# A two-half transformer layer on one core: from scheduled order to source order paced by an estimate

## The chip, the cores and the metric

The kernel runs on one core of a Trainium2 chip. The core has five engines that each work through a queue of their own: TensorE (PE in the profile: matmuls, with their weight loads shown apart as PEld), VectorE (DVE), ScalarE (ACT), GpSimd (POOL) and SyncE (SP, which here only issues transfers). An engine that reaches an instruction whose inputs aren't ready waits there, and everything behind it on the same queue waits too. The metric is device time in microseconds for one execution.

## What is computed

256 tokens of width 2048 pass through one layer of a hybrid decoder, all in f32:

```python
proj = rms_norm(x, g_mix_pre) @ w_in          # split into q, k, v, HGRN2 q/f/i/g and two gates
merged = sigmoid(gate_a) * (y_attn @ w_attn_branch) + sigmoid(gate_b) * (y_hgrn @ w_hgrn_branch)
x = x + rms_norm(merged @ w_out, g_mix_post)
gate, up = split(rms_norm(x, g_ffn_pre) @ w_gate_up)
x = x + rms_norm((silu(gate) * up) @ w_down, g_ffn_post)
ple_gate = sigmoid(rms_norm(x, g_ple_pre) @ w_ple_gate)
x = x + rms_norm((p @ w_ple_proj) * ple_gate, g_ple_post)
```

y_attn is sliding-window attention with sinks (16 heads, window 128), y_hgrn a gated linear recurrence (8 heads, chunks of 64). d_ff is 5632. Each weight matrix is read from HBM once, some 270 MB in all.

## The kernel before

The tokens are two halves of 128 (c = 0 and 1). The activations of a half are the stationary operand of a matmul, 128x128 and transposed, and the streamed weights are the moving one, 128x512. To keep f32 precision, every product is three matmuls in the fp32r format: xh·wh + xh·wl + xl·wh, where xh and wh are rounded values (`hi`, `wh`) and xl and wl the remainders (`lo`, `wl`). This gives 6192 "wide" matmuls and 584 small ones (128x128 transposes, the recurrence, the attention); the profile counts 814 small, since a product of plain f32 operands that isn't a transpose stands in it twice.

A weight **pair** is two chunks of 128 rows and 512 columns, 512 KB: SP loads it into one of 5 `raw` buffers, ACT writes `wh`, DVE writes `wl = raw - wh`; 8 pairs of split weights can be held. There are 516 pairs, each used by 12 wide matmuls, 6 for each half. `block` takes a slab of up to 8 pairs through half 0 (48 matmuls into one PSUM accumulator `acc`), then through half 1, then calls `evac`, which reads the accumulator on ACT or DVE.

The stages run in this order: 19 blocks of `w_in` (the mixer; the small matmuls of recurrence and attention stand among them), the two branch projections, `w_out`, `w_gate_up` in 11 pairs of blocks (ev_g and ev_u make `sg` = silu(gate)·up, which is transposed on PE into `actT`), `w_down`, and `w_ple_proj` with `w_ple_gate`. Three of the stages begin with a norm: at the start of the program, after w_out (the first norm boundary) and after w_down (the second). At a norm, `x` is updated on DVE, transposed on PE, multiplied by the gain into `hi` (ACT) and `lo` (DVE), and its sum of squares (ACT, `junk`) gives `rstd` (DVE, then a power on POOL). The scale by `rstd` is applied only when an accumulator of the next stage is read.

What sets the order: outside the first block the tile scheduler does. The source gives weight splits a higher priority (`AHEAD`) and the norms at the boundaries a higher one still (`URGENT`); PSUM is four `acc` banks, two `mt` and two `mh`. Only the first block's instructions are pinned in source order. There, x is loaded and transposed group by group (4 groups of 512 columns for each half), and a whole group is multiplied by its gains on DVE (`h`), rounded on ACT (`hi`) and subtracted on DVE (`lo`), each at 128x512.

Of the kernel before, what the change touches and what calls it, by code (L numbers as in the profile page):

```python
# [18 lines left out]
P = 128  # L19
# [8 lines left out]
AHEAD = 1000  # L28
URGENT = 3000
# [3 lines left out]
def block_kernel(ctx: ExitStack, tc: tile.TileContext, I, out: bass.AP):  # L33
    """256 tokens as two halves of 128 on the partitions; weights stream once.

    A product x @ w is xh@wh + xh@wl + xl@wh, with xh, wh the float32r
    roundings and xl, wl the remainders (exact in float32r).
    """
# [3 lines left out]
    wraw = ctx.enter_context(tc.tile_pool(name="wraw", bufs=5))  # L42
    wsplit = ctx.enter_context(tc.tile_pool(name="wsplit", bufs=8))
    psum = ctx.enter_context(tc.tile_pool(name="psum", bufs=4, space=bass.MemoryType.PSUM))

    V, A, G, T = nc.vector, nc.scalar, nc.gpsimd, nc.tensor
    count = [0]

# [4 lines left out]
    # 2 KB slots, handed out in the order of emission, the longest free first  # L53
# [14 lines left out]

    def acc():
        return psum.tile([P, NB], F32, tag="acc", name=nm("acc"))  # L70

    def misc(tag="mt"):
        return psum.tile([P, NB], F32, tag=tag, bufs=2, name=nm("misc"))

    pinned = [False]

    def kept(ins):
        return tc.keep_in_program_order(ins) if pinned[0] else ins

    def act(o, i, f, **kw):  # L80
        return kept(A.activation(o, i, f, **kw))  # L81

    def tt(o, a, b, op):
        return kept(V.tensor_tensor(o, a, b, op))  # L84

    def ts(o, a, s1, op0, s2=None, op1=None):
        if op1 is None:
            return kept(V.tensor_scalar(o, a, s1, None, op0))
        return kept(V.tensor_scalar(o, a, s1, s2, op0, op1))  # L89

    def stt(o, a, s, b, op0, op1):
        return kept(V.scalar_tensor_tensor(o, a, s, b, op0, op1))  # L92
# [8 lines left out]
    def weight_load(w, k, col):  # L101
        raw = wraw.tile([P, 2, NB], F32, tag="raw", name=nm("raw"))
        nc.sync.dma_start(
            raw, w[k * P:(k + 2) * P, col:col + NB].rearrange("(c p) n -> p c n", p=P))
        return raw

    def weight_split(raw):
        """hi and lo parts of two k-chunks."""
        hi = wsplit.tile([P, 2, NB], F32R, tag="wh", name=nm("wh"))
        lo = wsplit.tile([P, 2, NB], F32R, tag="wl", name=nm("wl"))  # L110
        act(hi, raw, AF.Copy)
        tt(lo, raw, hi.bitcast(F32), ALU.subtract)
        return [(hi[:, j, :], lo[:, j, :]) for j in range(2)]

    def weight_slab(w, ks, col):
        pairs = []
        for k in ks[::2]:
            raw = weight_load(w, k, col)
            with tc.high_priority(offset=AHEAD):
                pairs.append((k, weight_split(raw)))  # L120
        return pairs

    def products(ps, lhs, pairs, start=True, stop=True):
        n = len(pairs)
        for i, (k, parts) in enumerate(pairs):
            for j, (wh, wl) in enumerate(parts):
                xh, xl = lhs(k + j)
                T.matmul(ps, xh, wh, start=start and i == 0 and j == 0, stop=False)  # L128
                T.matmul(ps, xh, wl, start=False, stop=False)  # L129
                T.matmul(ps, xl, wh, start=False, stop=stop and i == n - 1 and j == 1)  # L130

    def block(w, ks, col, lhs, evac):
# [163 lines left out]
    for g in range(4):  # L296
        ahead = first_group(g + 1) if g < 3 else None
        if g == 1:
            lower_bounds()
# [623 lines left out]
```

## Time and profile before

| | |
|---|---|
| runs | 1552.91 us median of 3 (1552.19 to 1555.55) |
| profiled execution, first to last instruction | 1552.4 us |
| PE busy | 1516.8 us, 98% |
| weight loads busy | 1243.8 us, 80% |
| DVE busy | 889.8 us, 57% |
| ACT busy | 786.3 us, 51% |
| first wide matmul starts | 12.12 us |
| last wide matmul starts | 1542.06 us |

The profiled execution has no time of its own beside its span. The span lies inside the spread of the runs, 0.5 us below their median, so span and time are taken as one. The busy time of PE is modelled from pipelined matmuls that overlap (one is shown as 0.39 us long while the next starts 0.23 us later), so a slice with 98% busy can still hold lost time. What is lost is read from the starts: how many matmuls start in a stretch against how many could.

### The profile page before, as it was taken

The page shows a single profiled execution, that of the slowest core. Times are in us where ns is not written, and L with a number is a line of the kernel's source. Part 1 is how long each engine was busy: PE and PEld are TensorE (multiplying, and loading weights), DVE is VectorE, ACT ScalarE, POOL GpSimd, SP SyncE. Part 2 cuts the span into 40 slices and gives each one's busy share as a digit, 9 for nine tenths or more (in the row PEclk, how much of TensorE's full clock was granted, in tenths as well). Part 3 has the DMA queues.
Part 4 walks back from the last instruction along what each step waited for, and adds up shares of the span by engine and source line. Part 5 has one row for each costly group of instructions (what it writes and reads, how often), then busy time and mean ns, then how long its engine had stood idle before and what let it go on. Part 6 is the DMA issues. An engine that isn't in the chain of part 4 may idle for free.

```text
span 1552.4 us, 18678 instructions
## 1 busy us (share of the span) xinstructions
PE 1516.8 (98%) x7006; PEld 1243.8 (80%) x7006; DVE 889.8 (57%) x1228; ACT 786.3 (51%) x1052; POOL 24.4 (2%) x36
## 2 busy tenths in 40 slices
PE   7999999999999999999999999999999999999997
PEld 5778887887878888887888888888888888888886
DVE  6886748676445565556543553454446556654854
ACT  4755745555664433546443444344345545543852
POOL 2000000000000000000000000000000000000000
PEclk9999999999999999999999999999999999999998
DMA  7645454545336765545545654565565565755452
GB/s 245 230 135 191 129 197 139 187 129 196 110 109 210 247 211 173 193 153 196 200 162 180 217 174 168 200 219 180 172 215 190 190 195 180 246 184 179 171 179 98
DMA packets 146618, 282.54 MB, mean 182 GB/s; under 512 B 9136, under 2 KB 9600, under 8 KB 146528
## 3 DMA queue, kind: packets, MB, share of 16 engines
q1 hardware_dynamic: 145968, 280.33, 54.2%
q0 software_dynamic: 528, 1.01, 0.3%
q8 instruction: 55, 0.90, 0.2%
q14 instruction: 35, 0.29, 0.1%
q10 hardware_dynamic: 32, 0.01, 0.0%
HBM read 279.21 MB, written 2.10 MB: 181 GB/s over the span
## 4 chain that ended last, share of the span: by engine, by line
PE 83%; DMA 6%; ACT 4%; DVE 4%; issue 2%; POOL 0%; SPq 0%; POOLq 0%; ACTq 0%; DVEq 0%
PE acc L130 26%; PE acc L129 26%; PE acc L128 26%; DMA raw<-in_w_gate_up 3%; ACT wh L81 3%; PE misc L159 2%; DMA raw<-in_w_in 2%; DVE wl L84 2%; PE misc L478 1%; PE misc L599 1%; PE misc L617 1%; DVE sg L92 1%; DMA x<-in_x 1%; ACT junk L81 0%; DMA raw<-in_w_down 0%
## 5 line engine op out<-in xcount | busy, mean ns | idle before, releaser
L84 DVE TENSOR_TENSOR wl<-raw,wh 128x1024 fp32r<-128x1024 f32 x516 | 626.7, 1223 | 352.9 <-ACT wh L81 322.4
L129 PE MATMUL acc<-wl,hi 128*128 128x512 f32 x2064 | 809.7, 392 | 1.5 <-DVE wl L84 1.5
L128 PE MATMUL acc<-wh,hi 128*128 128x512 f32 x2064 | 809.4, 392 | 1.2 <-ACT hi L81 0.8
L130 PE MATMUL acc<-wh,lo 128*128 128x512 f32 x2064 | 809.1, 392 | 0.0
L81 ACT ACTIVATE wh<-raw 128x1024 fp32r<-128x1024 f32 x516 | 545.1, 1061 | 254.6 <-PE acc L130 182.1
L128 PEld LDWEIGHTS acc<-wh,hi 128*128 128x128 f32 x2064 | 388.1, 188 | 81.2 <-ACT hi L81 1.1
L129 PEld LDWEIGHTS acc<-wl,hi 128*128 128x128 f32 x2064 | 388.0, 188 | 80.9 <-DVE wl L84 2.1
L130 PEld LDWEIGHTS acc<-wh,lo 128*128 128x128 f32 x2064 | 388.0, 188 | 79.0 <-issue 0.5
L81 ACT ACTIVATE actT<-misc 128x512 f32<-128x512 f32 x22 | 13.2, 598 | 114.1 <-PE misc L159 114.1
L92 DVE SCALAR_TENSOR_TENSOR sg<-acc,rstd,sg 128x512 f32<-128x512 f32 x26 | 19.4, 747 | 77.4 <-PE acc L130 76.1
L81 ACT ACTIVATE sg<-acc,rstd 128x512 f32<-128x512 f32 x26 | 17.7, 681 | 84.1 <-PE acc L130 84.1
L84 DVE TENSOR_TENSOR lo<-actT,hi 128x512 fp32r<-128x512 f32 x44 | 30.2, 688 | 29.1 <-PE acc L129 22.1
L81 ACT ACTIVATE hi<-actT 128x512 fp32r<-128x512 f32 x44 | 27.4, 626 | 35.7 <-PE acc L130 29.8
L81 ACT ACT_TABLE_LOAD x30 | 38.5, 1283 | 2.1 <-PEq L911 1.2
L81 ACT ACTIVATE junk<-acc 128x512 bf16<-128x512 f32 x16 | 9.5, 596 | 56.2 <-DVE yg L84 56.2
L178 POOL TENSOR_TENSOR rstd<-mse,mhalf 128x1 f32<-128x1 f32 (+1 forms) x14 | 13.7, 979 | 1409.0 <-DVE mse L89 1409.0
L84 DVE TENSOR_TENSOR yg<-acc,gp 128x512 f32<-128x512 f32 x16 | 11.0, 686 | 42.7 <-PE acc L130 42.7
L81 ACT ACTIVATE xx<-xx 128x512 f32<-128x512 f32 (+1 forms) x28 | 16.7, 599 | 29.7 <-DVE xx L84 24.9
L81 ACT ACTIVATE gate<-acc,rstd 128x512 f32<-128x512 f32 x16 | 10.9, 681 | 35.1 <-PE acc L130 35.1
L605 DVE CUSTOM_DVE_ANT_0 s<-misc,amask 128x128 f32<-128x128 f32 (+1 forms) x32 | 10.1, 354 | 27.4 <-PE misc L599 27.4
L159 PE MATMUL misc<-ident,x 128*128 128x128 f32 x96 | 15.9, 296 | 8.8 <-DMA x<-in_x 6.7
L159 PEld LDWEIGHTS misc<-ident,x 128*128 128x128 f32 x96 | 11.6, 150 | 13.6 <-DMA x<-in_x 7.2
(157 smaller groups left out, 579.5 us busy)
## 6 DMA issues: line engine op xcount, KB each, us to landing
raw<-in_w_gate_up SPq DMA_DIRECT2D x176, 512.0 KB, 5.1
raw<-in_w_in SPq DMA_DIRECT2D x152, 512.0 KB, 5.1
raw<-in_w_down SPq DMA_DIRECT2D x88, 512.0 KB, 5.5
raw<-in_w_out SPq DMA_DIRECT2D x32, 512.0 KB, 5.5
raw<-in_w_ple_gate SPq DMA_DIRECT2D x32, 512.0 KB, 5.8
raw<-in_w_attn_branch SPq DMA_DIRECT2D x16, 512.0 KB, 5.9
raw<-in_w_hgrn_branch SPq DMA_DIRECT2D x16, 512.0 KB, 5.6
x<-in_x SPq DMA_DIRECT2D x16, 256.0 KB, 6.9
```

The costliest lines, as they stand in the source:

```text
L81: return kept(A.activation(o, i, f, **kw))
L84: return kept(V.tensor_tensor(o, a, b, op))
L92: return kept(V.scalar_tensor_tensor(o, a, s, b, op0, op1))
L128: T.matmul(ps, xh, wh, start=start and i == 0 and j == 0, stop=False)
L129: T.matmul(ps, xh, wl, start=False, stop=False)
L130: T.matmul(ps, xl, wh, start=False, stop=stop and i == n - 1 and j == 1)
L159: T.transpose(ps[:, cols(i)], src[:, cols(i)], ident)
L178: G.tensor_tensor(r, u, mhalf[:, :m], ALU.pow)
L478: T.matmul(ps[:, cols(h, 64)], xh, blk(xh)[:, :, 1, :], start=True, stop=True)
L599: T.matmul(ps[:, cols(i, nk * P)], qT[:, cols(j0 + i)], kTp[n][:, g, 0:nk * P], start=True, stop=True)
L605: V.tensor_tensor_reduce(s[:, cols(i, nk * P)], ps[:, cols(i, nk * P)], amask[:, (1 - c) * P:256], 1.0, NEG, ALU.add, ALU.max, mx[:, hb + ...
L617: T.matmul(y[:, cols(hb + i, 64)], pT[:, cols(i * nk + b)], vtok[:, b, kv:kv + 64], start=b == 0, stop=b == nk - 1)
```

## The change

Every instruction of every engine is now kept in the order in which the Python source emits it. The source emits in an order that it works out itself: a running clock counts 0.227 us for each wide matmul and 0.11 us for each small one, each of the other engines has an estimate of when it will be free, and everything that isn't a product of streamed weights is written as a generator that yields what it waits for (an engine, a tile, or a number of microseconds). A generator that is due by the clock is stepped between the matmuls (`pump`), or at once where something needs its result (`hurry`). Weight splits are paced too (`prefetch`): one pair at least 2.3 us after the last, up to 7 pairs ahead, up to 13 around the norm boundaries and in the ple stage.

Within a block the halves now alternate pair by pair: 6 matmuls for half 0, then 6 for half 1. Only at the two norm boundaries (last block before, first block after) and in the last block is half 1 six pairs behind half 0 (`LAG`), and while half 1 finishes the last block before a norm, splits beyond two pairs pause (`calm`). The 8 PSUM banks come from one pool. The products p @ w_ple_proj are computed first of all, stored to DRAM by POOL's queue (8 transfers of 256 KB) and read back through SP's queue after w_down. In the first block each group of x is now made by chunk: 4 times 128x128 `hi` on ACT, then 4 times `lo` on DVE, with no `h`. The order of some mixer blocks, the order of the three terms (xh·wh, xl·wh, xh·wl), and a few loads of ACT's tables ahead of their use change as well. The numbers of wide and small matmuls and of pairs stay as they were.

```diff
-AHEAD = 1000
-URGENT = 3000
+SPLIT, LOADED, PACE = 7, 5, 2.3
+EXTRA = 6
+LAG = 6
+WIDE, SMALL = 0.227, 0.11
+LATENCY = 0.2
...
+            start = max([clock[0], self.until] + [written.get(key(x), 0.0) for x in outs + ins])
+            self.until = start + us
+            for x in outs:
+                written[key(x)] = self.until + LATENCY
...
+                return tc.keep_in_program_order(f(o, *a, **kw))
...
+    V = InOrder(nc.vector, 0.08, 0.00105)
+    A = InOrder(nc.scalar, 0.16, 0.00095)
...
+    def step(gen):
+        to = next(gen, None)
+        if to is not None:
+            if to is T:
+                due = clock[0] + 0.2 + LATENCY
+            elif isinstance(to, InOrder):
+                due = max(clock[0], to.until) + LATENCY
+            elif hasattr(to, "shape"):
+                due = max(clock[0], written[key(to)])
+            else:
+                due = clock[0] + to
+            count[0] += 1
+            heapq.heappush(waiting, (due, count[0], gen))
...
+    def pump():
+        while waiting and waiting[0][0] <= clock[0]:
+            step(heapq.heappop(waiting)[2])
...
-    def block(w, ks, col, lhs, evac):
-        pairs = weight_slab(w, ks, col)
-        for c in range(2):
-            ps = acc()
-            products(ps, lhs[c], pairs)
-            evac(c, ps)
...
+    def prefetch():
+
+        while loaded and (len(ready) < 2 or (
+                not calm[0] and len(ready) + held[0] < depth[0] and clock[0] > paced[0])):
+            paced[0] = max(paced[0], clock[0] - PACE) + PACE
+            split_pair()
+            if plan:
+                load_pair()
...
+        for i in range(n + lag):
+            if lag and i in (lag, n):
+                calm[0] = i == n and last
+            if i < n:
...
+                use(0, i)
+                prefetch()
+                pump()
+            if i >= lag:
+                use(1, i - lag)
+                pairs[i - lag][1]()
+                held[0] -= 1
+                prefetch()
+                pump()
...
-            if not by_chunk:
-                h = slot("h")
-                tt(heads(h), heads(ps), gcol[:, c0:c0 + 4].unsqueeze(2).broadcast_to([P, 4, P]), ALU.mult)
-                self.groups.append(split(h))
...
+    prefetch()
+    for n in range(4):
+        stream([acc(), acc()], [p_lookup(0), p_lookup(1)], "w_ple_proj", [0, 1], n * NB, evac=ev_p(n))
+        if n in (0, 2):
+            add_xg(n // 2)
...
+    first = [acc(), acc()]
     for g in range(4):
+        for h in range(2):
+            stream(first, hT, "w_in", [4 * g + 2 * h, 4 * g + 2 * h + 1], 5 * NB, g + h == 0, g + h == 4)
+            if g in (1, 2) and h == 0:
+                add_xg(g + 1)
...
+        block("w_gate_up", K16, j * NB, h2T, ev_g, LAG * (j == 0))
+        depth[0] = SPLIT
+        block("w_gate_up", K16, DFF + j * NB, h2T, ev_u)
...
+    for n in range(4):
+        block("w_ple_gate", K16, n * NB, h3T, ev_s(n), LAG * (n in (0, 3)))
```

What moves is shown at three places in the order in which each engine has its instructions. The numbers in the names only tell buffers apart.

**The first block.** DVE, before: while the first block of w_in runs, the third group of x follows the splits `wl` of the second, each group as `h`, then `lo`.

```order
L84 TENSOR_TENSOR h_54_217<-misc_53_212,gcol_73 128x512
L84 TENSOR_TENSOR lo_56_220<-h_54_217,hi_55_219 128x512
L84 TENSOR_TENSOR wl_58_224<-raw_50_206,wh_57_223 128x1024
L84 TENSOR_TENSOR wl_60_228<-raw_51_208,wh_59_227 128x1024
L84 TENSOR_TENSOR h_62_236<-misc_61_231,gcol_73 128x512
L84 TENSOR_TENSOR lo_64_239<-h_62_236,hi_63_238 128x512
```

DVE after, at the third group of x (`lo_121` is of half 0, `lo_126` of half 1):

```order
L132 TENSOR_TENSOR wl_105_373<-raw_67_222,wh_104_372 128x1024
L132 TENSOR_TENSOR wl_108_385<-raw_75_253,wh_107_384 128x1024
L132 TENSOR_TENSOR wl_119_423<-raw_91_304,wh_118_422 128x1024
L132 SCALAR_TENSOR_TENSOR lo_121_428<-misc_110_390,gcol_104,hi_114_403 128x128 x4
L132 TENSOR_TENSOR wl_123_440<-raw_97_327,wh_122_439 128x1024
L132 SCALAR_TENSOR_TENSOR lo_126_446<-misc_112_395,gcol_104,hi_116_408 128x128 x4
L132 TENSOR_TENSOR wl_128_458<-raw_102_355,wh_127_457 128x1024
```

ACT after, at the same place:

```order
L132 ACTIVATE wh_107_384<-raw_75_253 128x1024
L132 ACTIVATE hi_114_403<-misc_110_390,gcol_104 128x128 x4
L132 ACTIVATE hi_116_408<-misc_112_395,gcol_104 128x128 x4
L132 ACTIVATE wh_118_422<-raw_91_304 128x1024
L132 ACTIVATE wh_122_439<-raw_97_327 128x1024
```

A group's `hi` for both halves now stands on ACT ahead of the next `wh`, and on DVE the `wl` of that pair stands ahead of the group's `lo`, while before `lo` stood ahead of the `wl`s.

**The transposes of sg in gate_up.** PE, before: `acc_1465` is the last accumulator of an up block (half 0), `acc_1468` that of the next block; `misc_1467` receives the four transposes of `sg_1438`.

```order
L130 MATMUL acc_1465_7142<-wh_1463_7138,lo_1146_5548 128x512
L128 MATMUL acc_1468_7199<-wh_1442_7096,hi_1164_5629 128x512
L129 MATMUL acc_1468_7199<-wl_1443_7097,hi_1164_5629 128x512
L130 MATMUL acc_1468_7199<-wh_1442_7096,lo_1165_5630 128x512
L128 MATMUL acc_1468_7199<-wh_1442_7096,hi_1164_5629 128x512
L129 MATMUL acc_1468_7199<-wl_1443_7097,hi_1164_5629 128x512
L159 MATMUL misc_1467_7193<-ident_71,sg_1438_7041 128x128 x4
L130 MATMUL acc_1468_7199<-wh_1442_7096,lo_1165_5630 128x512
```

PE after: `acc_1905` and `acc_1906` are the halves of an up block, `acc_1933` and `acc_1934` those of the next.

```order
L132 MATMUL acc_1905_7332<-wh_1907_7346,lo_1586_5853 128x512
L132 MATMUL acc_1905_7332<-wl_1908_7347,hi_1585_5848 128x512
L132 MATMUL acc_1906_7333<-wh_1907_7346,hi_1628_6014 128x512
L132 MATMUL acc_1906_7333<-wh_1907_7346,lo_1629_6019 128x512
L132 MATMUL acc_1906_7333<-wl_1908_7347,hi_1628_6014 128x512
L132 MATMUL acc_1906_7333<-wh_1907_7346,hi_1628_6014 128x512
L132 MATMUL acc_1906_7333<-wh_1907_7346,lo_1629_6019 128x512
L132 MATMUL acc_1906_7333<-wl_1908_7347,hi_1628_6014 128x512
L132 MATMUL acc_1933_7480<-wh_1910_7364,hi_1563_5762 128x512
```

and directly behind these rows:

```order
L132 MATMUL acc_1933_7480<-wh_1910_7364,lo_1564_5768 128x512
L132 MATMUL acc_1933_7480<-wl_1911_7365,hi_1563_5762 128x512
L132 MATMUL misc_1935_7485<-ident_74,sg_1900_7316 128x128 x4
L132 MATMUL acc_1933_7480<-wh_1910_7364,hi_1563_5762 128x512
L132 MATMUL acc_1933_7480<-wh_1910_7364,lo_1564_5768 128x512
L132 MATMUL acc_1933_7480<-wl_1911_7365,hi_1563_5762 128x512
L132 MATMUL misc_1937_7493<-ident_74,sg_1901_7324 128x128 x4
L132 MATMUL acc_1934_7481<-wh_1910_7364,hi_1593_5888 128x512
```

Before, the transposes stand 5 wide matmuls behind the last one of the half that they belong to. Now those of half 0 stand 9 behind it, those of half 1 6 behind it with the other group of four between.

**The second norm boundary.** ACT, before: `hi` of half 1's norm in pieces (`hi_2244`, `hi_2247`), the sigmoid `s_2295` of the first ple_gate block's half 0, and weight splits `wh`.

```order
L81 ACTIVATE hi_2241_11062<-misc_2240_11057,gcol_73 128x128 x2
L81 ACTIVATE hi_2244_11079<-misc_2243_11074,gcol_73 128x128
L81 ACTIVATE hi_2241_11062<-misc_2240_11057,gcol_73 128x128
L81 ACT_TABLE_LOAD
L81 ACTIVATE s_2295_11237<-acc_2294_11188,rstd_2227_10990 128x512
L81 ACTIVATE hi_2244_11079<-misc_2243_11074,gcol_73 128x128
L81 ACTIVATE hi_2247_11096<-misc_2246_11091,gcol_73 128x128
L81 ACTIVATE wh_2301_11300<-raw_2300_11298 128x1024
L81 ACTIVATE hi_2244_11079<-misc_2243_11074,gcol_73 128x128
L81 ACTIVATE hi_2247_11096<-misc_2246_11091,gcol_73 128x128
L81 ACTIVATE wh_2308_11324<-raw_2307_11322 128x1024
```

ACT after: `hi_2861` and `hi_2882` belong to half 1's norm, `s_2876` is the sigmoid of half 0, `junk` its sum of squares, which reads the product that DVE makes of it.

```order
L132 ACTIVATE wh_2857_11366<-raw_2778_11063 128x1024
L132 ACTIVATE hi_2861_11380<-misc_2860_11375,gcol_104 128x128 x4
L132 ACTIVATE wh_2864_11394<-raw_2781_11081 128x1024
L132 ACTIVATE wh_2873_11412<-raw_2785_11102 128x1024
L132 ACTIVATE s_2876_11424<-acc_2842_11292,rstd_2872_11407 128x512
L132 ACTIVATE junk_70,ess_2835_11288<-s_2876_11424 128x512
L132 ACTIVATE wh_2878_11436<-raw_2791_11121 128x1024
L132 ACTIVATE hi_2882_11447<-misc_2881_11442,gcol_104 128x128 x4
```

Before, ten instructions and more stand between the sigmoid and its sum of squares, and the rest of half 1's `hi` lies between. Now the sum of squares follows the sigmoid at once, and a split and the `hi` of a group of half 1 stand behind both.

## Rows read from the trace of the kernel before

**Rows 1.** The page: busy time of each engine.
```profile
PE 1516.8 (98%) x7006; PEld 1243.8 (80%) x7006; DVE 889.8 (57%) x1228; ACT 786.3 (51%) x1052; POOL 24.4 (2%) x36
```

**Rows 2.** The page: the chain that ended last, by engine.
```profile
PE 83%; DMA 6%; ACT 4%; DVE 4%; issue 2%; POOL 0%; SPq 0%; POOLq 0%; ACTq 0%; DVEq 0%
```

**Rows 3.** Windows, accumulators alone: PE, PEld, DVE, ACT busy (count), clock, DMA, GB/s.
```profile
0.00:25.00 25.00, 11.80 (x42) 8.56 (x43) 0.00 (x0) 0.00 (x0) 1.00 0.86 295
25.00:50.00 25.00, 21.88 (x91) 16.33 (x90) 0.00 (x0) 0.00 (x0) 1.00 0.72 231
50.00:519.00 469.00, 409.94 (x1695) 313.15 (x1694) 13.41 (x26) 24.58 (x37) 1.00 0.48 159
725.00:1200.00 475.00, 465.53 (x2028) 378.89 (x2027) 15.70 (x21) 14.28 (x21) 1.00 0.56 190
1250.00:1350.00 100.00, 100.00 (x443) 82.81 (x442) 2.74 (x4) 2.75 (x8) 1.00 0.63 203
1425.00:1475.00 50.00, 46.72 (x201) 36.97 (x200) 1.37 (x2) 5.53 (x12) 1.00 0.50 176
```

**Rows 4.** Windows, small matmuls' PSUM tiles alone; columns as in rows 3.
```profile
50.00:519.00 469.00, 85.69 (x593) 69.77 (x593) 37.58 (x97) 23.42 (x40) 1.00 0.48 159
725.00:1200.00 475.00, 13.20 (x84) 9.53 (x84) 0.34 (x1) 12.55 (x21) 1.00 0.56 190
```

**Rows 5.** Timeline of PE, start of the program: start, length, operation.
```profile
12.12 0.78 PE L128 MATMUL acc<-wh,hi 128*128 128x512 f32 x1
...
14.40 0.63 PE L128 MATMUL acc<-wh,hi 128*128 128x512 f32 x1
14.82 0.61 PE L129 MATMUL acc<-wl,hi 128*128 128x512 f32 x1
```

**Rows 6.** Groups by line and shape: busy us, mean ns | idle before, releaser.
```profile
L84 DVE TENSOR_TENSOR wl<-raw,wh 128x1024 fp32r<-128x1024 f32 x516 | 626.7, 1223 | 352.9 <-ACT wh L81 322.4 <-DMA x<-in_x 1.8
L81 ACT ACTIVATE wh<-raw 128x1024 fp32r<-128x1024 f32 x516 | 545.1, 1061 | 254.6 <-PE acc L130 182.1 <-DMA raw<-in_w_gate_up 24.6 <-DMA raw<-in_w_in 19.2
...
L81 ACT ACTIVATE hi<-misc,gcol 128x128 fp32r<-128x128 f32 x64 | 20.9, 373 | 2.9 <-DVE lo L92 2.8
...
L92 DVE SCALAR_TENSOR_TENSOR lo<-misc,gcol,hi 128x128 fp32r<-128x128 f32 x64 | 19.8, 344 | 4.2 <-ACT hi L81 3.9
...
L178 POOL TENSOR_TENSOR rstd<-mse,mhalf 128x1 f32<-128x1 f32 x10 | 7.4, 737 | 1146.1 <-DVE mse L89 1146.1
...
L84 DVE TENSOR_TENSOR s<-s,proj 128x512 f32<-128x512 f32 x6 | 4.1, 687 | 15.7 <-ACT s L81 15.7
L81 ACT ACTIVATE s<-acc,rstd 128x512 f32<-128x512 f32 x6 | 4.1, 680 | 13.9 <-PE acc L130 13.9
...
L81 ACT ACTIVATE junk<-s 128x512 bf16<-128x512 f32 x6 | 3.8, 630 | 0.0
```

**Rows 7.** Timeline of PE in gate_up, around one group of transposes.
```profile
1109.65 0.39 PE L129 MATMUL acc<-wl,hi 128*128 128x512 f32 x1
1110.31 0.66 PE L159 MATMUL misc<-ident,sg 128*128 128x128 f32 x4 [0.27 <-DVE sg L92]
...
1111.03 0.39 PE L128 MATMUL acc<-wh,hi 128*128 128x512 f32 x1
```

**Rows 8.** Waits of weight loads, 725 to 1200 us: total, times, longest.
```profile
PEld misc L159 <- DVE sg L92: 7.6, 11, 1.1
```

**Rows 9.** Timeline of PE at the second norm boundary.
```profile
1443.78 1.03 PE L159 MATMUL misc<-ident,x 128*128 128x128 f32 x8
...
1444.88 0.40 PE L128 MATMUL acc<-wh,hi 128*128 128x512 f32 x1
```

**Rows 10.** Timeline of all engines, end of the program.
```profile
1542.06 0.39 PE L130 MATMUL acc<-wh,lo 128*128 128x512 f32 x1
1542.49 0.84 ACT L81 ACTIVATE s<-acc,rstd 128x256 f32<-128x256 f32 x2 [8.86 <-PE acc L130]
...
1544.53 0.16 DVE L84 TENSOR_TENSOR u<-ess 128x1 f32<-128x1 f32 x1 [0.75 <-ACT junk L81]
```

More of the change, by code (lines that the diff above doesn't have):

```diff
@@ L1 @@
+import heapq
 import math
+from functools import partial
 from collections import deque
@@ L115, in weight_slab @@
[L115 to L130, printed above, removed]
@@ new lines, in stream, with use @@
+    def stream(pss, lhs, w, ks, col, start=True, stop=True, lag=0, evac=None, last=False):
+        n = len(ks) // 2
+        pairs = {}
+        def use(c, i):
+            k = ks[2 * i]
+            for j in range(2):
+                terms(pss[c], lhs[c], k + j, pairs[i][0][j], start and i == 0 and j == 0,
+                      stop and i == n - 1 and j == 1)
+                if j == 0:
+                    pump()
+            if evac and i == n - 1:
+                evac(c, pss[c])
+        for i in range(n + lag):
+            if lag and i in (lag, n):
+                calm[0] = i == n and last
+            if i < n:
+                what, *pairs[i] = ready.popleft()
+                assert what == (w, ks[2 * i], col), (what, w, ks[2 * i], col)
+                held[0] += 1
+                use(0, i)
[6 more added lines that the diff above has]
+                prefetch()
+                pump()
@@ L139, in lookup, with block, there @@
+    def block(w, ks, col, lhs, evac, lag=0, last=False):
+        stream([acc(), acc()], lhs, w, ks, col, lag=lag, evac=evac, last=last)
     def lookup(groups):
+        def there(g):
+            return g in groups if isinstance(groups, dict) else len(groups) > g and groups[g] is not None
         def f(k):
+            hurry(lambda: there(k // 4))
             hi, lo = groups[k // 4]
@@ L312, in block_kernel @@
+    r1 = [n.done() for n in norms]
     rope = [{}, {}]
@@ L527, in hgrn_core, with hgrn @@
         hg_o[c, g] = o, rstd(ss, 1, P, 4)
+    def hgrn(c):
+        for g in range(2):
+            yield from hgrn_core(c, g)
     def evac_hg(g):
@@ L626, in attention, with attend @@
         tt(heads(ya, 64), heads(y, 64), den.unsqueeze(2).broadcast_to([P, 8, 64]), ALU.mult)
-        yaT[c][n] = split(transpose4(ya))
+        drop(y)
+        yield V
+        ps = yield from transpose4(ya)
         free(ya)
+        yield T
+        yield from split(ps, yaT[c], n)
+        drop(ps)
+    def attend(n):
+        while n and yaT[1][0] is None:
+            yield 1.0
+        for c in range(2):
+            yield from attention(c, n)
     def mixer_block(col, evac):
-        block(w_in, K16, col * NB, hT, evac)
+        block("w_in", K16, col * NB, hT, evac)
     gates = {}
@@ L788, in act_parts, with f @@
-        return parts
-    def load_p():
-        p2 = I["p"].rearrange("l o (c p) d -> (l o c) p d", p=P)
-        t = slot("pin")
-        for c in range(2):
-            nc.sync.dma_start(t[:, cols(c, 256)], p2[c])
-        parts = split(transpose4(t))
-        free(t)
+        hurry(lambda: all(actT[c][j] is not None for c in range(2) for j in KGROUPS[gi]))
+        parts = [{}, {}]
+        def f():
+            for j in KGROUPS[gi]:
+                for c in range(2):
+                    yield from split(actT[c][j], parts[c], j)
+                    if pair == 1:
+                        free(actT[c][j])
+                    yield 1.0
@@ L797, in load_p @@
+        chain(f())
         return parts
```

768 lines of the change are left out of this document (513 added, 255 removed).

## Prediction

> **What bounds the kernel now.** I read the page first. PE is busy 98% of the span, DVE 57% and ACT 51% [rows 1], and the chain that ended last runs through PE for 83% [rows 2]. So TensorE is the bound, and what the other engines do costs time only where PE waits for them. Since PE's busy share says little about lost starts, I then counted wide matmuls by stage in the windows. Undisturbed, 443 start in 100 us, one per 0.226 us, at a granted clock of 1.00, the 2.4 GHz level [rows 3]. The 6192 wide ones need 6192 × 0.226 = 1399 us.
>
> For the small ones I take a price from the second norm boundary, where nothing waited: from the start of eight transposes to the second wide one behind them it is 1444.88 − 1443.78 = 1.10 us [rows 9]. Less one wide, that is 0.87 us for eight, 0.11 each, with the change between the kinds included. For the other 7006 − 6192 = 814 records of PE [rows 1] that makes 90 us. First wide start 12.12 us [rows 5], tail after the last wide start 1552.4 − 1542.06 = 10.3 us [rows 10]. Together 1399 + 90 + 12 + 10 = 1511 us; the other 41 us are waits, slow starts, and changes between kinds that cost more than this. I place them by stage:
>
> - 0 to 50 us: 42 + 91 = 133 wide [rows 3], 30 us of work. From 12.12 on there are 38 us, so 8 us are left, of which transposes take some 3: 5 us.
> - 50 to 519 us (mixer): 469 − 1695 × 0.226 − 593 × 0.11 = 469 − 383 − 65 = 21 us [rows 3, 4].
> - 725 to 1200 us (gate_up): 475 − 2028 × 0.226 − 84 × 0.11 = 475 − 458 − 9 = 8 us [rows 3, 4].
> - 1425 to 1475 us (second norm boundary): 50 − 201 × 0.226 − 32 × 0.11 = 1 us [rows 3].
>
> That is 35 of the 41 us; the rest lies between these stretches. The DMA share is 0.48 to 0.63 in the steady stages [rows 3], so transfers aren't the bound there.
>
> **The change part by part.** The span serves as the profiled execution's time: 1552.4 us, 0.5 us below the median of 1552.9.
>
> *The number of matmuls* is unchanged, and so are the weight splits: 12 wide use 12 × 0.226 = 2.72 us of PE for each pair, against 1.06 us on ACT and 1.22 us on DVE [rows 6]. A pace of 2.3 us is quicker than PE's use, so the depth fills. Cost 0, covered by PE; if a queue were blocked for longer than the depth of 7 pairs (19 us), the cover would be gone.
>
> *Start.* p and one weight pair land first, so wide matmuls can begin at about 8.5 us instead of 12.1 (an estimate: the first split follows the first pair as it does before). The 48 of p's projection stand ahead of the first block, whose 96 are then held by its order. For the third group of x, from its transposes to the first matmul that reads its `lo`, PE has some 13 wide, 2.95 us. On ACT stand 4 `hi`, 4 `hi`, and `wh`. In the group row a `hi` is 0.37 us long, and back to back they take 20.9 / 64 = 0.33 each, so 1.3 + 1.3 + 1.06 us; then `wl` 1.22 and the first `lo` 0.31 on DVE [rows 6]: 5.2 us, so PE waits 2.3 us. Half 1's `lo` stands behind a further `wl`, for another 1.1 us. With the fourth group the same again: 6.8 us. PE then ends p's projection and this block near 8.5 + 144 × 0.226 + 16 transposes and changes (2 to 3 us) + the slow first starts and the pace of landing weights (about 4 us) + 6.8 = 54.5 us. Before had 133 wide by 50 us, so 144 near 52.5 to 53. Net **+1 us** after the four transposes of p, which are done already. The bounds are −6 (no wait occurs) and +8 (the other two groups are held too). The eight stores (2 MB in all) on POOL's queue meet the stretch with DMA share 0.86 [rows 3]; at 295 GB/s they are 7 us of transfer, but weights land faster there than PE uses them, so I take nothing. POOL itself is busy 2% [rows 1].
>
> *Mixer.* All chains of recurrence and attention are laid out by the estimate. A step on DVE is estimated too short, by 1.22 against 0.08 + 1024 × 0.00105 = 1.16 us for `wl`, and PE's clock too fast, because it knows no change between kinds. The second error works for the kernel: an instruction is emitted on PE later than its inputs are ready. So I count that most waits go, and in the order of instructions 147 groups of small matmuls have become 127 in the whole program. Bounds: 0 (each wait is replaced by another) and −21. I take **−11**, the middle, since a group that stands alone costs more in changes between kinds than my price from a group of eight, and most of these groups stay.
>
> *Branches and w_out*: −0.3, a few transposes further back.
>
> *gate_up.* From 1109.65 to 1111.03 us stand four transposes and two wide: 1.38 − 0.45 = 0.93 us for four, against 4 × 0.11 = 0.44 unhindered, so 0.49 lost to the wait for `sg` [rows 7]. Such waits are listed 11 times [rows 8]: 11 × 0.49 = 5.4. With nine matmuls between instead of five they have 2.0 us instead of 1.1, and the wait needed 0.3 to 0.7 us more. I take **−4.7**, since not each loses as much; bounds −8 and 0.
>
> *First norm boundary*: half 1 is six pairs behind, so half 0's norm has 36 wide, 8 us, and then half 1's norm runs under the next block's start. Taken as **0**; bounds −2 and +7 (as at the second). *Start of w_down*: the first splits of actT stand behind the last sg, **+1**.
>
> *Second norm boundary.* ACT's queue has `s`, then `junk`, then `wh` and the four `hi` of half 1. `s` waits for rstd, which comes from sums of squares through DVE and a 0.74 us power on POOL; with the steps between engines some 1.9 us. Then `s` 0.68, the product on DVE 0.69, `junk` 0.63, and two passes between engines: 2.5 us more [rows 6]. Behind this wait `wh` and `hi` that PE needs next: about 4.5 us, and by the same walk two smaller waits of 0.7 and 1.6 us for earlier groups. 6.8 us in place of 1 to 2: **+5**; bounds 0 and +8.
>
> *Tail.* Before, both `s` go first: 2.04 us from `s` to `u` [rows 10]. Now `s`, `junk`, `s`, `junk` alternate with DVE between: **+1.2**. The reading back of p's projection is 2 MB on SP's queue with 13 pairs split ahead: 0.
>
> Sum: 1 − 11 − 0.3 − 4.7 + 0 + 1 + 5 + 1.2 = **−7.8 us**, so 1544.6 on the span and 1545 beside the median.
>
> **The rivals.** *A, the queues hold PE (slower).* An in-order queue lets one late instruction stop all behind it, at all four groups of x and at both boundaries. Price: 3.4 us for each of two more groups and +7 at the first boundary, 14 us above my sum: **1559 us**. It decides once the extra waits exceed 8 to 11 us. For it speaks that ACT and DVE have fixed orders now; against it that elsewhere they are half idle [rows 1].
>
> *B, the waits that I walked don't occur.* Without the 6.8 us in the first block and the 5 at the boundary: 1545 − 11.8 = **1533 us**. For it: PE may already be late at these places, so that its wait is spread.
>
> *C, waits are only exchanged (no effect).* The mixer's gain of 11 is eaten by new waits, from estimates that are 5% short, and the second boundary costs half of what I walked: 1545 + 11 − 2.5 = **1554 us**. For it: what is lost now is a few tenths at each of many places, and 5% of a chain of several steps is as much.
>
> *D, the clock.* Accumulators now change every 6 matmuls instead of every 24 to 48. If PE idled between them so that the clock fell, wide matmuls would start further apart; at the start of the program they do, 0.42 us from 14.40 to 14.82 [rows 5], though the row of that stretch shows 1.00. 5% of 6192 at 0.2 more each is 62 us: **1607 us**. Against it: the clock is 1.00 in all windows [rows 3], among them w_down, where four accumulators are in turn, and no row shows a loss there.
>
> The Trainium skill ("TensorE: Matmul & The Clock Gate", "A second HAM failure mode: psum-queue depth-cycling") tells of a kernel that cycled through PSUM banks in each iteration, idled a little between groups of matmuls, and swung between the two clock levels. By that, this change would end at rival D. No run here shows it yet.
>
> **How the numbers follow.** My forecast (1540 to 1550) has 0.50, A 0.12, B 0.18, C 0.17, D 0.03. Within 0.2%, 3.1 us, is about what a measurement of this kernel can tell from no change: 1549.8 to 1556.0. Forecast and B give faster, 0.68; C gives same, 0.17; A and D slower, 0.15. The range reaches to B's 1533 less 4 for the mixer, and to A's 1559: 1529 to 1559, with D and the outer parts of A and B left out.
>
> **What would show it.** The windows of accumulators: by 50 us fewer wide starts than 133 if the first block waits, some 126; in the mixer's stretch 0.5 us per 50 us more starts; in gate_up no wait of transposes for `sg`; after the last w_down a gap of 4 to 5 us on PE that ends with `hi` or `wh` on ACT; a tail of 11.5 us. I am wrong if PE runs through the second boundary without a gap, if waits in the mixer remain as they are, or if the clock leaves 1.00.

## Result and the profile after

The changed kernel takes 1541.72 us (median of 4 runs, 1540.03 to 1542.28) beside 1552.55 us for the kernel before. The ratio is 0.9919, with a 95% interval of 0.9902 to 0.9935: 10 to 15 us faster. The span of the profiled execution fell from 1552.4 to 1539.6 us, by 12.8 us. That execution itself took 1541.63 us, so 2.0 us lie outside its span. Ahead of the prediction, span and time of the kernel before were taken as one; in later runs of that kernel, too, the time is about 1.8 us longer than the span (1554.02 beside 1552.1, for one). Its profiled execution was thus some 1.7 us above the median, which is why the spans differ by 2 us more than the medians. Spans are compared with spans below.

The page after: engines, the granted clock, and the chain that ended last (answering to [rows 1, 2]).

```profile
PE 1511.7 (98%) x7006; PEld 1251.5 (81%) x7006; DVE 882.7 (57%) x1266; ACT 786.3 (51%) x1099; POOL 28.1 (2%) x44
...
PEclk9999999999999999999999999999999999999998
...
PE 94%; DVE 1%; DMA 1%; ACT 1%; issue 1%; SPq 0%; POOL 0%; POOLq 0%; DVEq 0%; ACTq 0%
```

The chain now lies on PE for 94% instead of 83%: the steps through ACT, DVE and DMA on which PE depended are nearly gone. The busy shares say nothing of it, for PE is at 98% in both.

Where the time came from is seen when the windows are cut at stage borders. First the kernel before, accumulators on PE alone (length, busy, number of starts, clock, DMA share, GB/s): first block; rest of the mixer; branches and w_out; gate_up; w_down; ple. A border may count a neighbour's first matmul.

```profile
0.00:39.43 39.43, 25.09 (x96) 1.00 0.75 247
39.43:519.20 479.77, 418.73 (x1729) 1.00 0.49 163
519.20:700.77 181.57, 176.84 (x769) 1.00 0.61 201
700.77:1198.18 497.41, 485.88 (x2113) 1.00 0.56 188
1198.18:1441.27 243.09, 240.19 (x1057) 1.00 0.61 196
1441.27:1542.29 101.02, 99.28 (x433) 1.00 0.46 156
```

Then the kernel after: p's projection; first block; and on as above.

```profile
0.00:22.75 22.75, 13.78 (x48) 1.00 0.90 315
22.75:52.21 29.46, 23.53 (x97) 1.00 0.86 298
52.21:517.22 465.01, 415.01 (x1729) 1.00 0.54 167
517.22:696.55 179.33, 177.03 (x769) 1.00 0.65 209
696.55:1188.37 491.82, 485.75 (x2113) 1.00 0.61 187
1188.37:1430.39 242.02, 240.59 (x1056) 1.00 0.63 203
1430.39:1528.59 98.20, 91.74 (x384) 0.97 0.42 137
```

The same 1728 wide matmuls of the mixer take 465.0 us instead of 479.8, which is −14.8. Branches and w_out: 179.3 from 181.6, −2.2. Gate_up with the first norm boundary: 491.8 from 497.4, −5.6. W_down −1.1. Against this, the start: 52.2 us, where before 39.4 and p's 48 wide matmuls and four transposes in the ple stage (11.3 by the prices of the prediction) make 50.7, +1.5. The ple stage with the second boundary: 98.2, where 101.0 − 11.3 = 89.7 would be the same, **+8.5**. The tail behind the last wide: 11.0 from 10.1, +0.9. Sum −12.8, the difference of the spans.

Waits of PE after (total, times, longest):

```profile
PE acc L132 <- DVE lo L132: 7.6, 7, 2.4
...
PE acc L132 <- ACT hi L132: 2.7, 2, 2.3
PE acc L132 <- ACT wh L132: 2.5, 1, 2.5
...
PE misc L132 <- DVE sg L132: 0.4, 1, 0.4
...
PEld misc L132 <- DVE sg L132: 0.6, 1, 0.6
```

The last line is of the weight loads: their waits for `sg` have shrunk to one of 0.6 us, from eleven with 7.6 us in gate_up alone [rows 8]. What is left are the wait for the first `wh` of all and waits for `lo` and `hi`. Four of those for `lo` stand in the first block and one (1.1 us) at the start of w_down; the others, with both for `hi`, stand at the second boundary. The experiments take the first block and the second boundary one by one.

The second boundary, timeline of ACT:

```profile
1447.76 0.69 ACT L132 ACTIVATE s<-acc,rstd 128x512 f32<-128x512 f32 x1 [3.01 <-POOL rstd L132]
1449.20 0.63 ACT L132 ACTIVATE junk<-s 128x512 bf16<-128x512 f32 x1 [0.76 <-DVE s L132]
...
1449.83 1.04 ACT L132 ACTIVATE wh<-raw 128x1024 fp32r<-128x1024 f32 x1
1450.78 1.12 ACT L132 ACTIVATE hi<-misc,gcol 128x128 fp32r<-128x128 f32 x4
```

Timeline of DVE there, the sum from which rstd is made:

```profile
1445.83 0.15 DVE L132 TENSOR_REDUCE ms<-ss 128x1 f32<-128x4 f32 x1
```

Timeline of PE at the same place:

```profile
1448.51 0.39 PE L132 MATMUL acc<-wl,hi 128*128 128x512 f32 x1
1451.18 0.50 PE L132 MATMUL acc<-wh,hi 128*128 128x512 f32 x1 [2.28 <-ACT hi L132]
1453.11 0.80 PE L132 MATMUL acc<-wh,lo 128*128 128x512 f32 x1 [1.43 <-DVE lo L132]
...
1454.13 0.63 PE L132 MATMUL acc<-wh,hi 128*128 128x512 f32 x1
1454.56 0.63 PE L132 MATMUL acc<-wh,lo 128*128 128x512 f32 x1
```

Windows of PE's accumulators there (after the count: clock, DMA share, GB/s):

```profile
1448.00:1451.00 3.00, 0.90 (x4) 1.00 0.76 244
1451.00:1454.00 3.00, 1.39 (x3) 0.75 0.26 82
1454.00:1458.00 4.00, 4.00 (x10) 0.50 0.71 217
```

ACT stands for 3.01 us at the sigmoid `s` until rstd is there, then waits for DVE's product, and only then makes the `wh` and `hi` behind them. That rstd is late has a cause of its own: `ms` starts on DVE at 1445.83, directly behind a `wl`, an `x`, a `lo` and another `wl`, though the last sum of squares that it adds ended on ACT at 1440.88. No run moved it. PE has nothing from 1448.9 to 1451.2 and waits again until 1453.1. Then something happens that my sum lacked: for about 4 us the granted clock is 0.50, the 1.2 GHz level, from 1454 to 1458, and wide matmuls start 0.43 us apart. Ten of them cost 0.2 us more each, 2 us.

### The profile page after: what moved, and what is told of

Same layout as the page of the kernel before. It is cut to its first block, busy times and chain, and to the rows that moved or that the text cites. A ratio compares the mean times of both kernels' runs of the same rounds, so it can differ in the third digit from the quotient of the medians.

```text
span 1539.6 us, 18701 instructions
## 1 busy us (share of the span) xinstructions
PE 1511.7 (98%) x7006; PEld 1251.5 (81%) x7006; DVE 882.7 (57%) x1266; ACT 786.3 (51%) x1099; POOL 28.1 (2%) x44
## 4 chain that ended last, share of the span: by engine, by line
PE 94%; DVE 1%; DMA 1%; ACT 1%; issue 1%; SPq 0%; POOL 0%; POOLq 0%; DVEq 0%; ACTq 0%
PE acc L132 89%; PE misc L132 6%; DMA raw<-in_w_ple_proj 1%; DMA raw<-in_w_in 1%; ACT hi L132 1%; DVE wl L132 1%; DVE lo L132 0%; ACT wh L132 0%; SPq L132 0%; ACT junk L132 0%; DVE eg L132 0%; DVE s L132 0%; ACT s L132 0%; DVE x L132 0%; POOL rstd L132 0%
## 5 line engine op out<-in xcount | busy, mean ns | idle before, releaser
L132 DVE TENSOR_TENSOR wl<-raw,wh 128x1024 fp32r<-128x1024 f32 (+1 forms) x534 | 625.0, 1187 | 511.1 <-ACT wh L132 502.5
L132 PE MATMUL acc<-wh,hi 128*128 128x512 f32 x2064 | 818.6, 397 | 5.2 <-ACT hi L132 2.7
L132 ACT ACTIVATE wh<-raw 128x1024 fp32r<-128x1024 f32 (+1 forms) x534 | 538.3, 1029 | 446.7 <-PE acc L132 400.4
L132 ACT ACTIVATE hi<-misc,gcol 128x128 fp32r<-128x128 f32 x96 | 26.9, 374 | 21.6 <-PE misc L132 21.5
L132 DVE SCALAR_TENSOR_TENSOR lo<-misc,gcol,hi 128x128 fp32r<-128x128 f32 x96 | 26.9, 344 | 13.9 <-ACT hi L132 13.8
L132 PEld LDWEIGHTS misc<-xx 128*128 128x128 f32 (+1 forms) x192 | 21.1, 173 | 4.1 <-issue 2.5
L132 DVE TENSOR_TENSOR gate<-acc,gate 128x512 f32<-128x512 f32 x16 | 11.1, 692 | 18.6 <-PE acc L132 18.6
L132 PE MATMUL misc<-xx 128*128 128x64 f32 (+1 forms) x192 | 21.4, 254 | 0.0
```

The source lines that it names most:

```text
L132: return tc.keep_in_program_order(f(o, *a, **kw))
```

## The experiments

All are set against the kernel before on the same chip by their ratio; the changed kernel's is 0.9919. Time is read by stage from the spans' windows, for these tell more than the ratios: in the runs that leave a stage alone it mostly repeats to 0.1 us (the mixer is 465.0 us in six runs, branches and w_out are 179.3 in seven). Only the start varies: the first block ends between 52.1 and 54.0 us in runs with the same start. The ratios of thin, lag4_all and extra3 have intervals that touch or overlap the changed kernel's (0.9902 to 0.9935), so what those three cost is read from the stages alone.

| run | median us | ratio (95% interval) | span us |
|---|---|---|---|
| late_sig | 1535.41 | 0.9882 (0.9866 to 0.9899) | 1533.1 |
| first_lo | 1535.28 | 0.9878 (0.9864 to 0.9893) | 1532.9 |
| combo | 1530.09 | 0.9829 (0.9816 to 0.9843) | 1528.1 |
| p_end | 1533.06 | 0.9851 (0.9838 to 0.9865) | 1531.8 |
| no_pace | 1810.52 | 1.1650 (1.1633 to 1.1667) | 1808.3 |
| thin | 1545.73 | 0.9937 (0.9918 to 0.9957) | 1543.1 |
| before_alt | 1550.74 | 0.9975 (0.9966 to 0.9984) | 1548.7 |
| lag4_all | 1546.90 | 0.9940 (0.9927 to 0.9954) | 1546.2 |
| extra3 | 1547.89 | 0.9950 (0.9935 to 0.9966) | 1545.6 |
| lag0 | 1571.96 | 1.0101 (1.0087 to 1.0114) | 1568.7 |

**late_sig: the sigmoid out of the norm's way.**

```diff
         def f(c, ps):
+            while n == 0 and norm3[1].groups[3] is None:
+                yield 0.3
             yield from norm3[c].ready()
```

> The changed kernel with one edit: at the second norm boundary the first sigmoid of half 0 is emitted only once all four groups of half 1's norm are done. My theory: the 8.5 us that the ple stage lost in the changed kernel come from ACT standing at this sigmoid until rstd is there, with half 1's hi behind it, and from the clock at 0.50 afterwards. Then PE has no gap above 1 us after the last w_down, the clock stays at 1.00 there, and the time is 1541.7 - 7 = 1535 us (1533 to 1537). Rival: the norm of half 1 itself is too slow for six pairs of lag, and the wait only comes elsewhere: 1540 to 1543 us.

The span is 6.5 us shorter. The ple stage, windows as above:

```profile
1430.35:1522.10 91.75, 89.20 (x384) 1.00 0.45 146
1447.00:1450.00 3.00, 2.79 (x13) 1.00 0.71 214
```

It takes 91.75 us instead of 98.2, at a clock of 1.00 throughout. So the sigmoid at the head of ACT's queue made the gap, and without the gap the clock doesn't fall. My theory holds; the 2 us that remain over 89.7 are shorter waits for `hi` and `lo`.

**first_lo: lo ahead of the next wl.**

```diff
             lo = self.hi(g, ps)
-            yield A
             lo()
```

> The changed kernel with one edit: in the first block lo of a group of x is emitted right behind hi, so DVE has it ahead of the next wl. My theory: the four waits of PE for lo in the first block, 2.5 + 0.7 + 1.5 + 0.7 = 5.3 us beyond the usual spacing, go: 1541.7 - 5 = 1537 us (1535 to 1539). Rival: wl then comes late by as much, or a landing weight sets the pace there: 1540 to 1543 us.

The first block:

```profile
23.11:46.69 23.58, 22.32 (x97) 1.00 0.89 322
```

It takes 23.6 us instead of 29.5 (96 wide are 21.7; in the other runs without this edit and with the same start it takes 28.4 to 28.9), and everything behind keeps the gain: the span is 6.7 us shorter. The four waits were what the order showed, `lo` behind a `wl` whose `wh` stood behind the other half's `hi`.

**combo: both, and the old order at the end.**

```diff
                 tt(s[:, sl], s[:, sl], proj[c][n][:, sl], ALU.mult)
-                square_sum(ess[c][:, n + i:n + i + 1], s[:, sl], w)
+            for i in range(m):
+                square_sum(ess[c][:, n + i:n + i + 1], s[:, cols(i, w)], w)
```

> The changed kernel with late_sig's edit, first_lo's edit, and at the program's end both products s before both sums of squares, as in the kernel before. If the three losses are independent of one another: 1541.7 - 6 - 6 - 1 = 1528.5 us (1527 to 1531). If the first block's earlier end only makes a later wait longer: 1533 to 1535.

The span is 11.5 us under the changed kernel's, and its tail 10.2 us. The first block keeps 23.6 us and the ple stage 91.7, as in the single runs. The losses were independent, though a start 1.6 us later than in the changed kernel (24.3 us for p's projection instead of 22.8, and not touched by the edits) hides a part. It is the fastest kernel of this study: 0.9829 of the kernel before.

**p_end: p's projection back in the ple stage,** on first_lo: no store, no load, each of its four blocks ahead of a ple_gate block.

```diff
     for n in range(4):
+        stream([acc(), acc()], [p_lookup(0), p_lookup(1)], "w_ple_proj", [0, 1], n * NB, evac=ev_p(n))
         block("w_ple_gate", K16, n * NB, h3T, ev_s(n), LAG * (n in (0, 3)))
```

> The kernel of first_lo with p's projection moved back to the ple stage, each of its blocks ahead of a ple_gate block, and no store to or load from DRAM. Set against first_lo (1535.3). My theory: p first fills time in which PE would wait for x and its norm, 4 us; back at the end its first block gives 2.7 us of matmuls under the second norm: 1536 to 1538 us. Rival 1: p first is the part that matters at the start, since the clock's slow first matmuls fall on it: 1539 to 1543. Rival 2: it makes no difference where p's products stand and the stores cost something: 1531 to 1534.

```profile
0.00:39.68 39.68, 23.32 (x96) 1.00 0.81 272
1419.12:1520.82 101.70, 100.00 (x432) 1.00 0.42 135
```

The start loses what I expected: 39.7 + 11.3 = 51.0 us against first_lo's 46.7, 4.3 us. But the ple stage, 101.7 − 11.3 = 90.4 us against first_lo's 97.0, gains 6.6, at a clock of 1.00. The 12 wide matmuls ahead of the first ple_gate block push the sigmoid back: in ACT's timeline the `hi` of half 1's third group now stands ahead of it (1434.1 us), and when it comes (1437.6) it waits for PE and no longer for rstd. So I was wrong on the sum, and the time, 1533.06, lies in rival 2's range: p first is not a gain of this change by itself. It gains 4 us at the start and takes away the cover of the second norm, which late_sig gives back in another way.

**no_pace: due at once.**

```diff
-EXTRA = 6
+EXTRA = 4
...
-                due = clock[0] + 0.2 + LATENCY
+                due = clock[0]
...
-                due = max(clock[0], to.until) + LATENCY
+                due = clock[0]
...
-                due = max(clock[0], written[key(to)])
+                due = clock[0]
```

> The changed kernel with the estimate taken out of the pacing: a generator that waits for an engine or a tile is due at once, at the next gap between products; only waits given as a number of us stay. Splits go up to 4 pairs further ahead instead of 6 around the norms, because buffers run out otherwise. My theory: the mixer's and gate_up's gain comes from emitting PE's small matmuls only when their inputs are ready by the estimate. Then the mixer's rest (now 8 us) and gate_up's (now 2 us) come back and more, since in order nothing can move ahead of a wait: 20 to 60 us slower than the changed kernel, 1562 to 1600 us. Rival: the gain is from alternating halves and from evenly paced splits, and the estimate only needs to be roughly there: 1540 to 1548 us.

Windows of the mixer's accumulators, then PE's longest waits in the whole run and its timeline in the mixer:

```profile
47.95:716.60 668.65, 405.04 (x1729) 0.82 0.37 117
```

```profile
PE misc L132 <- DVE xx L132: 66.0, 23, 5.0
```

```profile
301.09 1.94 PE L132 MATMUL misc<-xx 128*128 128x64 f32 x8 [3.00 <-DVE xx L132]
305.84 1.94 PE L132 MATMUL misc<-xx 128*128 128x64 f32 x8 [2.81 <-DVE xx L132]
```

The mixer alone takes 668.7 us, 204 more than paced, and its clock is 0.82. The direction is as expected, the size over four times the upper end (269 us on the medians): I had counted waits of a few tenths, but they reach 5.0 us. The steps of recurrence and attention now stand on PE's queue one behind the other, with no wide matmul between them, as the two rows show. The mixer's 593 small matmuls stand in 13 groups instead of 77. PE's waits there come to 127 us, and the small matmuls themselves are busy for 141 us instead of 80, since the clock is low where they stand alone (0.50 from 300 to 325 us); counted from the starts, the wide ones behind one another lose only 8 us more. So what is lost is the work that covered each step, and with it the clock of the small ones. Source order that emits everything at once loses 16%, then. That the estimate is what wins is shown only against this extreme: a fixed distance in matmuls, without an estimate, wasn't tried.

**thin: the estimate half a microsecond too early.**

```diff
-LATENCY = 0.2
+LATENCY = -0.3
```

> The changed kernel with LATENCY = -0.3 instead of 0.2, so each generator that waits for an engine or a tile is due 0.5 us earlier, with the estimate otherwise as it is. Without pacing the kernel lost 257 us on the kernel before, so this asks how exact the estimate must be. If margins are as thin as I took them (0.3 to 0.5 us at sg's transposes), PE waits a few tenths at most steps: the mixer's rest goes from 8 to 20 or 40 us, gate_up's from 2 to 6: 1557 to 1580 us. If the time between two pumps (0.7 us) and the changes between kinds that the clock leaves out already cover half a microsecond: 1540 to 1546 us.

```profile
51.23:520.06 468.83, 411.97 (x1729) 1.00 0.54 166
...
702.06:1196.14 494.08, 485.39 (x2113) 1.00 0.62 186
1440.72:1532.02 91.30, 88.12 (x385) 1.00 0.42 139
```

The time, 1545.7 us, lies in the rival's range, but two things cancel in it. The mixer takes 3.8 us more (468.8) and gate_up 2.3 (494.1); w_out and w_down, where transposes of the norm's x now wait, 2.6 each. That is 11.3 us, nearly the 12.8 of the whole change. The ple stage is 6.9 us shorter, since half 1's norm is emitted earlier there, ahead of the sigmoid as in late_sig, and the clock stays at 1.00; the start gives another 1. So half a microsecond matters wherever it isn't offset by a repair of the second boundary. Whether a margin set apart for norms and mixer would have both gains wasn't tried.

**before_alt: alternating halves in the scheduled kernel.**

```diff
-        for c in range(2):
-            ps = acc()
-            products(ps, lhs[c], pairs)
-            evac(c, ps)
+        pss = [acc(), acc()]
+        for i, pair in enumerate(pairs):
+            for c in range(2):
+                products(pss[c], lhs[c], [pair], i == 0, i == len(pairs) - 1)
+        for c in range(2):
+            evac(c, pss[c])
```

> The kernel before with one edit: in each block of eight pairs (w_down aside) the halves alternate pair by pair, 6 matmuls each, and both accumulators are read at the end; the tile scheduler still sets the order. My theory: alternating by itself brings nothing, 1552.5 us plus or minus 4 (later reads of half 0 may even cost some). Rival: alternating is what gives evac chains their distance, and most of the gain: 1540 to 1546 us. If the clock suffered from accumulators that change every 6 matmuls, it would show here too, as a granted clock under 1.00.

```profile
39.75:512.65 472.90, 421.04 (x1729) 1.00 0.55 170
696.38:1190.46 494.08, 487.87 (x2113) 1.00 0.61 187
```

Time falls by 0.25%, inside what I expected, but for a reason that I hadn't: the mixer gains 6.9 us (472.9) and gate_up 3.3 (494.1), and the tail loses 4.0 (14.1), since both halves end together, and w_out about 3, where PE waits 4.2 us for x at the first boundary. So alternating is worth about half of the mixer's gain even where the scheduler sets the order. The clock is 1.00 over both stages with accumulators that change every 6 matmuls; only behind two waits of PE, of 2.5 and 4.2 us, is it at 0.50 for some 3 us.

**lag4_all: halves four pairs apart in the mixer and in gate_up.**

```diff
-        block("w_in", K16, col * NB, hT, evac)
+        block("w_in", K16, col * NB, hT, evac, 4 * (col != 2))
...
-        block("w_gate_up", K16, j * NB, h2T, ev_g, LAG * (j == 0))
+        block("w_gate_up", K16, j * NB, h2T, ev_g, LAG if j == 0 else 4)
...
-        block("w_gate_up", K16, DFF + j * NB, h2T, ev_u)
+        block("w_gate_up", K16, DFF + j * NB, h2T, ev_u, 4)
```

> The changed kernel with half 1 four pairs behind half 0 in all blocks of w_in but the one for keys and values, and in all of gate_up, so the halves alternate in half of a block only; the estimate paces as before. In the scheduled kernel alternating brought 7 us in the mixer and 3 us in gate_up. If alternating is worth that by itself, much of it is given back here: 1546 to 1552 us. My theory: once instructions are placed by the estimate, the order of the halves doesn't matter: 1540 to 1544 us.

```profile
53.97:520.35 466.38, 411.26 (x1729) 1.00 0.53 163
699.71:1192.30 492.59, 486.34 (x2113) 1.00 0.59 186
```

The time, 1546.9, lies in the first theory's range, 1546 to 1552, but not for its reason. In the edited stages 1.4 and 0.8 us are given back, little of the 10 that alternating brought under the scheduler; another 2.3 us appear in w_down, right behind gate_up, and 1.7 at the start, which the edit doesn't touch. Under the estimate, then, the order of the halves matters by 2 to 5 us. The dose is half, for the halves still alternate in four of a block's eight pairs.

**extra3 and lag0: depth and lag at the norms.**

```diff
-EXTRA = 6
+EXTRA = 3
```

and for lag0 besides

```diff
-LAG = 6
+LAG = 0
```

> The changed kernel with EXTRA = 3 instead of 6 and LAG as it is; it is the control for lag0, which has both edits. If the lag alone carries the boundaries: 1541.7 plus or minus 2. If depth matters: ACT must do three more splits while it makes hi, 3 us at each boundary, and some of it reaches PE: 1544 to 1550 us.

> The changed kernel with LAG = 0, so the halves alternate pair by pair at the norm boundaries too (EXTRA is 3 instead of 6, because buffers run out otherwise). My theory: six pairs of lag, 8 us of matmuls, cover the chain from a half's last accumulator over rstd, x and its transposes to the first hi, some 7 us. Without it PE waits that long at each boundary, its clock falls afterwards as it did at the second boundary (2 us), and the program's end gets 3 to 4 us longer, since both halves end together: 20 to 30 us over the changed kernel, 1562 to 1572 us. Rival: the depth of split weights is what carries the boundaries, and the lag is of little worth: 1540 to 1546 us.

Extra3, gate_up (with the first boundary) and ple:

```profile
696.72:1192.68 495.96, 486.99 (x2113) 1.00 0.62 189
1434.76:1534.64 99.88, 91.94 (x384) 0.97 0.42 132
```

Lag0 at the first boundary, timeline of PE:

```profile
694.88 0.39 PE L132 MATMUL acc<-wl,hi 128*128 128x512 f32 x1
700.74 1.11 PE L132 MATMUL misc<-ident,x 128*128 128x128 f32 x4 [5.47 <-DVE x L132]
702.31 0.80 PE L132 MATMUL acc<-wh,hi 128*128 128x512 f32 x1 [0.46 <-ACT hi L132]
```

Three pairs less depth cost 4.2 us at the first boundary and 1.7 at the second: 6.0 us, where ACT and DVE make splits while they should make `hi` and `lo`. Without the lag, 23 us more come on top (1568.7 − 1545.6): PE waits 5.5 us for x at a boundary, then several times about 1 us for each group, and the tail is 16.1 us. Of the 23 us, 5 are the tail's and 18 the boundaries', in w_out, gate_up and w_down. Lag and depth both carry the boundaries, the lag three times as much.

## Why the prediction was right

The direction, the range and the main steps hold. 1545 was forecast and 1541.7 measured; on the spans, −7.8 and −12.8 us. Term by term:

- *Start*, +1: +1.5. The waits for `lo` were forecast as 2.3 + 1.1, twice, and are 2.5, 0.7, 1.5 and 0.7 beyond the usual spacing; first_lo shows that their cause is the one named. The first wide starts at 7.68 us, not 8.5. That only 126 would start by 50 us was wrong, for this stretch holds 136 (58 and 78 in the windows of 25 us): the first block ends at 52.2 us and not at 54.5, 1.5 us of it by shorter waits and 0.8 by the earlier start. That the term fits all the same is partly luck, since I had set 54.5 against 52.5 to 53 for the kernel before, where the same work takes 39.4 + 11.3 = 50.7.
- *Mixer*, −11: −14.8. I took the middle of 0 to −21, which was too little. Counted from the starts, the stage's small matmuls, with the changes to and from them, take 71.5 us instead of 83.7; that is 12.2 of the 14.8. My reason for holding back, that a small group pays more for its changes than a group of eight, fails for groups of four: the four transposes at 1440.30 us hold the wide ones up by 0.44 us, 0.11 each. Source order emitted at once doesn't bring the gain, as no_pace shows, though its blocks and halves come in the same order and its splits at the same pace; alternating brings 6.9 of it even under the scheduler, as before_alt shows. How the rest divides between the estimate, the evenly paced splits, the new order of blocks and that of the three terms stays open.
- *Branches and w_out*, −0.3: −2.2. I had counted no waits there; I didn't test this term.
- *gate_up and first boundary*, −4.7 and 0: −5.6 together. The reason, transposes that stand further behind `sg`, is seen in the waits; alternating under the scheduler brings 3.3 of it (before_alt).
- *w_down*, +1: −1.1. The wait at its start is there (0.6 and 1.1 us on PE), but counted from the starts the 12 transposes inside the stage take 1.3 us, where before 16 took 3.7.
- *Second boundary*, +5: +8.5. The mechanism is the one of the prediction, sigmoid first and `hi` behind; late_sig shows it. What failed is the size: 2.4 + 1.7 + 0.8 + 0.9 = 5.8 us of waits instead of 6.8, and the fall of the clock, 2 us and more, that the sum didn't have. The 1 to 2 us that I set off for the kernel before were too much as well: by my own prices its ple stage lost 101.0 − 432 × 0.226 − 24 × 0.11 = 0.7.
- *Tail*, +1.2: +0.9.

The two mis-sized terms, mixer and second boundary, had errors of 3.8 and 3.5 us that offset each other, which is luck; the net miss of 5 us comes from the small terms.

Of the signs that I named, gate_up's came true but for one wait of 0.4 us. The gap at the second boundary came as two, 2.3 us that ended with `hi` and 1.4 with `lo`, and the tail is 11.2 us, counted as in the prediction (11.5). One sign of being wrong came true in one place: the clock left 1.00 there. The sign for the mixer, 0.5 us per 50 us, didn't follow from my term: 11 us in 469 are 1.2 per 50, and 14.8 are 1.5.

Of the rivals, A and B fell: no other group of x holds PE, nor does the first boundary, and the walked waits did occur. C fell with the mixer. D, too: wide matmuls start 0.23 us apart at a clock of 1.00 in all long stages, and in before_alt outside a few us behind two waits. The rule of the Trainium skill ("TensorE: Matmul & The Clock Gate", "A second HAM failure mode: psum-queue depth-cycling") isn't contradicted by that, since it blames idle time between groups, and here PE hardly idled between them: where it did, for 2.3 and 1.4 us at the second boundary, the clock fell to 0.50.

## What to carry to other kernels

In this kernel, source order paid with a model that says when each input is ready: emitted at once, it lost 16%, with the model it gained 0.8%. Half a microsecond of error in the model cost 11 us in four stages, which a lucky repair elsewhere mostly hid, so read such a test stage by stage. Before such an order is built, read each engine's queue at the places where stages meet, and ask of every instruction there what it waits for and which needed one stands behind it: three edits of a line or two were worth nearly as much again (11.5 us of span) as the whole change. Work that looks free to move (p's projection) may be the cover of a wait elsewhere, so price both places.

## What the runs showed of the hardware

- After a gap of 2.3 us and another of 1.4 us with one wide matmul between them, the granted clock stood at 0.50 for about 4 us of full work, with wide matmuls 0.43 us apart instead of 0.23. In lag0, where the gap was 5.5 us, the first wide matmuls behind it took the slow spacing as well. Single gaps of nearly the same length had either sequel. PE in the first block of the changed kernel, then in before_alt:

```profile
37.29 0.50 PE L132 MATMUL acc<-wh,lo 128*128 128x512 f32 x1 [2.36 <-DVE lo L132]
37.63 0.39 PE L132 MATMUL acc<-wl,hi 128*128 128x512 f32 x1
```

```profile
44.26 0.79 PE L128 MATMUL acc<-wh,hi 128*128 128x512 f32 x1 [2.54 <-ACT hi L81]
44.85 0.63 PE L129 MATMUL acc<-wl,hi 128*128 128x512 f32 x1
45.28 0.63 PE L130 MATMUL acc<-wh,lo 128*128 128x512 f32 x1
```

  The first was followed at once by matmuls 0.23 us apart at 1.00, the second by six 0.43 us apart at 0.50. So a gap on PE can be dearer than its length (at the second boundary, 3.7 us of gaps cost another 2 us in wide matmuls), but its length alone doesn't tell here whether it is.
- A power on POOL that computes rstd took from 0.55 to 1.48 us in either kernel (0.55 at 1433.43 us and 1.48 at 699.70 before, 1.48 at the second boundary after); the 0.74 us of [rows 6] is a mean of such values. Nothing here settles why.
